# Two interleavings in a one-core hybrid layer: RWKV's triangular inverse for two tiles in step, and SSD's second state product and transposes back in another place

## The chip, the cores and the metric

The kernel runs on one core of a Trainium2 chip. The metric is the device time of one execution in microseconds; the time before is the median of three runs. The engines are TensorE (PE, with its weight loads shown apart as PEld), VectorE (DVE), ScalarE (ACT), GpSimd (POOL) and SyncE (SP), which here issues most DMAs.

## The reference, cut to what matters

One layer with three parallel token mixers on x of 256 tokens by 2048 channels, all in float32. Each mixer reads one combined projection of x; the branches are gated, merged, projected and normalised. The change touches two of the mixers:

```python
def ssd_chunked(xh, dt, a, bm, cm):              # 8 groups, 2 chunks of 128 tokens
    ...
    cb = jnp.einsum('bclgn,bcsgn->bcgls', cc, bc)
    y_diag = jnp.einsum('bcgls,bgjcls,bcsgjp->bclgjp', cb, lmat, x)
    ...
    states = jnp.einsum('bclgn,bgjcl,bclgjp->bcgjpn', bc, decay_states, x)
    ...
    y_off = jnp.einsum('bclgn,bcgjpn,bgjcl->bclgjp', cc, states, jnp.exp(cs))
    return (y_diag + y_off).reshape(b, s, h, p)

def rwkv7_recurrence(r, w, k, v, a, bvec):       # 16 heads of 64, one step for each token
    def step(state, inp):
        r_t, w_t, k_t, v_t, a_t, b_t = inp
        sa = jnp.einsum('bhvk,bhk->bhv', state, a_t)
        state = (state * w_t[:, :, None, :] + sa[..., None] * b_t[:, :, None, :]
                 + v_t[..., None] * k_t[:, :, None, :])
        return state, jnp.einsum('bhvk,bhk->bhv', state, r_t)
```

In SSD, the group's y is then multiplied with silu(z), normalised over the group's 256 channels and scaled.

## The kernel before, in words

Every large product is split into three: the weights arrive as float32 halves of 512 KB (raw), ACT rounds them to hi (L344), VectorE forms lo (L346), and TensorE adds hi*xhi, hi*xlo and lo*xhi in PSUM (L417 to L419 in proj, 48 matmuls of 128x256 for a column tile). These projections form a nearly unbroken stream on TensorE, in the order of two hand-written lists, PROG (RWKV, gates, u) and PROG2 (SSD, S5, the branches). All other products of the mixers are put between them by the Tile scheduler, which orders each engine's instructions by priority (the order of the program, or above it with high_priority) as they become ready in its own timing; on the chip each engine then follows that order. issue_after adds an edge: what it covers is issued behind a given instruction of the same engine.

RWKV works on 16 heads in four batches; a batch has two tiles (i) of two heads (h), 256 tokens in four chunks of 64. For each chunk a unit triangular 64x64 matrix is inverted. Its 32x32 diagonal blocks are inverted on VectorE (rwkv_tinv, 31 steps), go through DRAM (Td) and come back as TTf (L685). The off-diagonal block is made of three steps on TensorE, each copied out of PSUM by ACT: rwkv_ty1 transposes one diagonal block into py (L698), rwkv_ty2 copies it to Y (L709), multiplies with Aoff (L712), copies (L713), multiplies with the other diagonal block (L716), and copies into TTf (L717). py is one PSUM tile, one bank, for each i; the scheduler keeps TensorE and ACT apart on the same bank, in program order. Before the change Y has one buffer, so tile 1 follows tile 0. rwkv_chunks then walks through the four chunks (L731, X by L733, L735, L737, L741 and so on).

SSD works on eight groups (S0 to S7 in PROG2). ssd_group projects xs0, xs1, B and C, convolves them on VectorE, and then makes: cb = B*C and a transpose of B (p1), xt, the transposes of xs (p2), the state st = BT*xdec (p3, first half, L924), copied to ST by ACT (L926), the product C*ST (p3, second half, L927), read by VectorE into off, the products y of the masked M with xdt (p4, L942), the gate and the norm on VectorE and ACT (L945 to L955), and yT, four transposes of y (p6, L959), which ACT scales into ya (L961). p1, p2, p3, p4 and p6 come in this order from one PSUM ring, tag "s", of two buffers.

Of the kernel before, what the change touches and what calls it, by code (L numbers as in the profile page):

```python
# [8 lines left out]
F32 = mybir.dt.float32  # L9
F32R = mybir.dt.float32r  # L10
AF = mybir.ActivationFunctionType
ALU = mybir.AluOpType
# [4 lines left out]
T = 256  # L17
# [187 lines left out]
def emit(tc, I, O, parts=("rwkv", "s5", "ssd", "final"), dbg=None):  # L205
    nc = tc.nc
    ctx = ExitStack()
    with ctx:
# [23 lines left out]
        for st in PROG:  # L232
# [6 lines left out]
            elif st[0] == "T":  # L239
                rwkv_tinv(g, bts[int(st[1:])], int(st[1:]))  # L240
            elif st[0] == "Y":
                b = int(st[1:])
# [201 lines left out]
NCH = T // CL  # L444
# [244 lines left out]
HS = [(slice(64 * h, 64 * h + 32), slice(64 * h + 32, 64 * h + 64)) for h in range(2)]  # L689
# [11 lines left out]


def rwkv_ty2(g, bt, b, pys):
    nc, rp = g.nc, g.rp
    for i in range(2):
        py = pys[i]
        Y = rp.tile([128, 2, NCH, 32], F32, name=f"Yl{b}_{i}", tag="Yl", bufs=1)
        for lo, hi in HS:
            nc.scalar.activation(Y[lo, 0], py[lo, 0], AF.Copy)  # L709
        for lo, hi in HS:  # L710
            for c in range(NCH):
                nc.tensor.matmul(py[hi, 1, c, :], lhsT=bt.Aoff[lo, i, c, :], rhs=Y[lo, 0, c, :], start=True, stop=True)  # L712
            nc.scalar.activation(Y[hi, 1], py[hi, 1], AF.Copy)  # L713
        for h, (lo, hi) in enumerate(HS):
            for c in range(NCH):
                nc.tensor.matmul(py[lo, 2, c, :], lhsT=Y[hi, 1, c, :], rhs=bt.TTf[hi, h, i, c, 32:64], start=True, stop=True)  # L716
            nc.scalar.activation(bt.TTf[lo, h, i, :, 32:64], py[lo, 2], AF.Copy)  # L717


def rwkv_chunks(g, bt, b):  # L720
# [68 lines left out]
LC = 128  # L789
# [62 lines left out]
def ssd_z(g, zp):  # L852

    nc = g.nc
    ps = [g.pp.tile([128, 512], F32, name=f"zq{zp}_{tk}", tag="pj", bufs=3) for tk in range(2)]
    for kb in range(4):
        hi, lo = g.loadw(g.I["wza"][4 * zp + kb], f"za{zp}_{kb}")
        for k in range(4):
            kk = 4 * kb + k
            f0, l0 = kk == 0, kk == NK - 1  # L860
            for tk in range(2):
                t = slice(128 * tk, 128 * tk + 128)
                nc.tensor.matmul(ps[tk], lhsT=g.xhi[:, kk, t], rhs=hi.k512(k), start=f0, stop=False)  # L863
                nc.tensor.matmul(ps[tk], lhsT=g.xhi[:, kk, t], rhs=lo.k512(k), start=False, stop=False)  # L864
                nc.tensor.matmul(ps[tk], lhsT=g.xlo[:, kk, t], rhs=hi.k512(k), start=False, stop=l0)  # L865
    g.zs = g.cz(f"zs{zp}")
    with g.tc.high_priority():
        for tk in range(2):
            nc.scalar.activation(g.zs[:, tk, :], ps[tk], AF.Tanh, scale=0.5)
            nc.vector.scalar_tensor_tensor(g.zs[:, tk, :], g.zs[:, tk, :], 1.0, ps[tk], ALU.add, ALU.mult)  # L870


def ssd_group(g, gr):
    nc, tc = g.nc, g.tc
    cv = []
    for n, t in (("xs0", 2 * gr), ("xs1", 2 * gr + 1), ("B", 16 + gr), ("C", 24 + gr)):
        ps = g.proj(f"x{t}")
        a = g.cv(f"{n}_{gr}")
        with tc.high_priority():
            nc.scalar.activation(a, ps, AF.Identity, scale=g.p("cw", 96 + t), bias=g.p("cb", t))  # L880
            for d in (1, 2, 3):
                nc.vector.scalar_tensor_tensor(a[:, d:T], ps[:, 0:T - d], g.p("cw", 32 * (3 - d) + t), a[:, d:T], ALU.mult, ALU.add)
        th = g.kp.tile([128, T], F32, name=f"th{n}_{gr}", tag="th", bufs=2)
        nc.scalar.activation(th, a, AF.Tanh)
        nc.vector.scalar_tensor_tensor(a, th, 1.0, a, ALU.add, ALU.mult)
        cv.append(a)
    if gr % 2 == 0:
        ssd_z(g, gr // 2)
    zs = g.zs[:, :, 256 * (gr % 2):256 * (gr % 2) + 256]
    xs, B, C = cv[0:2], cv[2], cv[3]  # L890
    idn = g.c("ident")
    hs = slice(4 * gr, 4 * gr + 4)
    csb = []
    for c in range(2):
        t = g.k2(f"csb{c}_{gr}", (128, 4, LC))
        nc.sync.dma_start(t, g.csd[hs, LC * c:LC * c + LC].unsqueeze(0).to_broadcast([128, 4, LC]))
        csb.append(t)

    p1 = g.pp.tile([128, 3, LC], F32, name=f"cb{gr}", tag="s", bufs=2)
    for c in range(2):  # L900
        w = slice(LC * c, LC * c + LC)
        nc.tensor.matmul(p1[:, c, :], lhsT=B[:, w], rhs=C[:, w], start=True, stop=True)
    nc.tensor.transpose(p1[:, 2, :], B[:, 0:LC], idn)
    BT = g.k1(f"BT{gr}", (128, LC))
    nc.scalar.activation(BT, p1[:, 2, :], AF.Copy)
    CBm = g.k1(f"CBm{gr}", (128, 2, LC))
    nc.vector.tensor_tensor(CBm, p1[:, 0:2, :], g.c("mC").unsqueeze(1).to_broadcast([128, 2, LC]), ALU.mult)

    p2 = g.pp.tile([128, 2, 4, 64], F32, name=f"xt{gr}", tag="s", bufs=2)
    for c in range(2):  # L910
        for q in range(2):
            nc.tensor.transpose(p2[:, c, 2 * q:2 * q + 2, :].rearrange("p a b -> p (a b)"), xs[q][:, LC * c:LC * c + LC], idn)
    xdt = g.k2(f"xdt{gr}", (128, 2, 4, 64))
    nc.vector.tensor_tensor(xdt, p2, g.csT[:, 1, :, hs].unsqueeze(3).to_broadcast([128, 2, 4, 64]), ALU.mult)
    y = g.k2(f"y_{gr}", (128, 2, 4, 64))
    nc.vector.tensor_tensor(y, p2, g.dskb[:, hs].unsqueeze(1).unsqueeze(3).to_broadcast([128, 2, 4, 64]), ALU.mult)
    dec = g.kp.tile([128, 4], F32, name=f"dec{gr}", tag="dec", bufs=2)
    nc.vector.tensor_tensor(dec, csb[0][:, :, LC - 1], g.csT[:, 0, 0, hs], ALU.subtract)
    nc.scalar.activation(dec, dec, AF.Exp)
    xdec = g.k1(f"xdec{gr}", (128, 4, 64))  # L920
    nc.vector.tensor_tensor(xdec, xdt[:, 0], dec.unsqueeze(2).to_broadcast([128, 4, 64]), ALU.mult)

    p3 = g.pp.tile([128, 2, T], F32, name=f"st{gr}", tag="s", bufs=2)
    nc.tensor.matmul(p3[:, 0, :], lhsT=BT, rhs=xdec.rearrange("p a b -> p (a b)"), start=True, stop=True)  # L924
    ST = g.k1(f"ST{gr}")
    nc.scalar.activation(ST, p3[:, 0, :], AF.Copy)  # L926
    nc.tensor.matmul(p3[:, 1, :], lhsT=C[:, LC:T], rhs=ST, start=True, stop=True)  # L927
    off = g.k1(f"off{gr}", (128, 4, 64))
    nc.vector.tensor_tensor(off, p3[:, 1, :].rearrange("p (a b) -> p a b", a=4), g.ecs[:, hs].unsqueeze(2).to_broadcast([128, 4, 64]), ALU.mult)
    nc.vector.tensor_tensor(y[:, 1], y[:, 1], off, ALU.add)  # L930

    M = csb
    for c in range(2):
        E = csb[c]
        for h in range(4):
            nc.scalar.activation(E[:, h, :], E[:, h, :], AF.Relu, scale=-1.0, bias=g.csT[:, 0, c, 4 * gr + h:4 * gr + h + 1])
        nc.scalar.activation(E, E, AF.Exp, scale=-1.0)
        nc.vector.tensor_tensor(E, E, CBm[:, c, :].unsqueeze(1).to_broadcast([128, 4, LC]), ALU.mult)
    p4 = g.pp.tile([128, 2, 4, 64], F32, name=f"y{gr}", tag="s", bufs=2)
    for c in range(2):  # L940
        for h in range(4):
            nc.tensor.matmul(p4[:, c, h, :], lhsT=M[c][:, h, :], rhs=xdt[:, c, h, :], start=True, stop=True)  # L942

    y = y.rearrange("p c a b -> p c (a b)")
    nc.vector.tensor_tensor(y, y, p4.rearrange("p c a b -> p c (a b)"), ALU.add)  # L945
    nc.vector.tensor_tensor(y, y, zs, ALU.mult)
    ss = g.kp.tile([128, 2], F32, name=f"ss{gr}", tag="ss", bufs=2)
    sq = g.k1(f"sq{gr}")
    for c in range(2):
        nc.scalar.activation(sq, y[:, c, :], AF.Square, accum_out=ss[:, c:c + 1])  # L950
    rs = g.kp.tile([128, 2], F32, name=f"rs{gr}", tag="rs", bufs=2)
    nc.scalar.activation(rs, ss, AF.Sqrt, scale=1.0 / 256, bias=g.ssdeps)
    nc.vector.reciprocal(rs, rs)
    for c in range(2):
        nc.scalar.activation(y[:, c, :], y[:, c, :], AF.Identity, scale=rs[:, c:c + 1])  # L955
    p6 = g.pp.tile([128, 2, T], F32, name=f"yT{gr}", tag="s", bufs=2)
    for q in range(2):
        for c in range(2):
            nc.tensor.transpose(p6[:, q, LC * c:LC * c + LC], y[:, c, 128 * q:128 * q + 128], idn)  # L959
    for q in range(2):  # L960
        nc.scalar.activation(g.ya[2 * gr + q], p6[:, q, :], AF.Identity, scale=g.p("nw", 2 * gr + q))  # L961

# [427 lines left out]
```

## Time and profile before

| | |
|---|---|
| median of 3 runs | 1308.43 us (1305.89 to 1310.21) |
| profiled execution, its own time | 1302.54 us |
| its span, first to last instruction | 1300.6 us |
| TensorE busy | 1268.7 us (98%), 10916 matmuls |
| TensorE weight loads busy | 1195.2 us (92%) |
| VectorE busy | 995.7 us (77%) |
| ACT busy | 768.5 us (59%) |
| mean granted TensorE clock | 0.997 |
| chain that ended last | PE 80%, DVE 7%, ACT 6%, DMA 3% |

Matmuls overlap in the pipeline, so the duration of one (0.28 us for 128x256) is longer than the distance from its start to the next one's; for what a matmul costs in a stream, starts are to be compared. An f32 product counts as two matmul instructions. In the rows, "x8" is the number of instructions merged into one row, and a bracket tells the idle time of the engine before the row and what ended it.

### The profile page before, as it was taken

What the parts mean: (1) busy time and instruction counts of PE and PEld (TensorE: products, weight loads), DVE (VectorE), ACT (ScalarE), POOL (GpSimd) and SP (SyncE); (2) the same over time, 40 slices, a digit from 0 to 9 for tenths busy, and PEclk for the clock granted to TensorE, in tenths of its full rate; (3) what the DMA queues carried; (4) which work ended last, traced back from release to release, by engine and by line L of the source; (5) the groups of instructions that cost most, each with busy time, mean ns of one, the idle gap of its engine ahead of it and who ended that gap; (6) DMA issues with size and microseconds to landing.
All of it is one profiled execution on the core that took longest, in us unless ns stands there. A gap on an engine that the chain in (4) does not pass through costs nothing.

```text
span 1300.6 us, 27378 instructions
## 1 busy us (share of the span) xinstructions
PE 1268.7 (98%) x10916; PEld 1195.2 (92%) x10916; DVE 995.7 (77%) x1823; ACT 768.5 (59%) x1379; POOL 14.8 (1%) x72
## 2 busy tenths in 40 slices
PE   8999999999999999989999999999999999999996
PEld 8999999999989889889989989999999999999885
DVE  6779987669959857889999867999597565448655
ACT  6676555577555657885756766766454454444530
POOL 2000000000000000000000000000000000000000
PEclk9999999999999999999999999999999999999998
DMA  8655655444564554555555556456655656677751
GB/s 313 181 169 173 187 174 167 139 124 145 166 177 152 168 183 132 159 186 164 178 163 180 170 178 195 146 158 192 193 171 164 193 179 211 209 230 243 255 167 65
DMA packets 97039, 230.71 MB, mean 177 GB/s; under 512 B 26736, under 2 KB 41616, under 8 KB 96912
## 3 DMA queue, kind: packets, MB, share of 16 engines
q1 hardware_dynamic: 96336, 227.60, 57.1%
q8 instruction: 86, 1.41, 0.5%
q10 hardware_dynamic: 576, 1.36, 0.3%
q14 instruction: 41, 0.34, 0.1%
HBM read 224.37 MB, written 3.24 MB: 175 GB/s over the span
## 4 chain that ended last, share of the span: by engine, by line
PE 80%; DVE 7%; ACT 6%; DMA 3%; issue 2%; SPq 1%; DVEq 0%; POOL 0%; ACTq 0%; POOLq 0%
PE ps_g L418 6%; PE ps_g L417 6%; PE ps_g L419 6%; PE br L1235 4%; PE br L1234 4%; PE br L1236 4%; PE ps_x L417 3%; PE ps_x L418 3%; PE ps_x L419 3%; PE po L1337 2%; PE po L1338 2%; PE po L1339 2%; PE zq L865 2%; PE zq L864 2%; PE zq L863 2%
## 5 line engine op out<-in xcount | busy, mean ns | idle before, releaser
L417 PE MATMUL ps_g<-xhi,hi_g 128*128 128x256 f32 x768 | 215.2, 280 | 0.0
L418 PE MATMUL ps_g<-xlo,hi_g 128*128 128x256 f32 x768 | 215.1, 280 | 0.0
L419 PE MATMUL ps_g<-xhi,lo_g 128*128 128x256 f32 x768 | 213.8, 278 | 0.0
L346 DVE TENSOR_TENSOR lo_g<-raw_g,hi_g 128x1024 fp32r<-128x1024 f32 x96 | 117.5, 1224 | 66.6 <-ACT hi_g L344 61.9
L344 ACT ACTIVATE hi_g<-raw_g 128x1024 fp32r<-128x1024 f32 x96 | 101.5, 1058 | 93.8 <-PE ps_g L418 71.4
L418 PEld LDWEIGHTS ps_g<-xlo,hi_g 128*128 128x128 f32 x768 | 144.6, 188 | 2.0 <-issue 1.0
L417 PEld LDWEIGHTS ps_g<-xhi,hi_g 128*128 128x128 f32 x768 | 144.6, 188 | 0.9
L417 PE MATMUL ps_x<-xhi,hi_x 128*128 128x256 f32 x512 | 144.6, 282 | 0.6 <-ACT sq L950 0.6
L419 PEld LDWEIGHTS ps_g<-xhi,lo_g 128*128 128x128 f32 x768 | 144.2, 188 | 0.5
L418 PE MATMUL ps_x<-xlo,hi_x 128*128 128x256 f32 x512 | 143.9, 281 | 0.0
L419 PE MATMUL ps_x<-xhi,lo_x 128*128 128x256 f32 x512 | 143.6, 280 | 0.0
L344 ACT ACTIVATE hi_b<-raw_b 128x1024 fp32r<-128x1024 f32 x64 | 67.8, 1059 | 75.8 <-PE br L1235 43.9
L346 DVE TENSOR_TENSOR lo_x<-raw_x,hi_x 128x1024 fp32r<-128x1024 f32 x64 | 78.3, 1223 | 27.1 <-ACT hi_x L344 27.1
L417 PEld LDWEIGHTS ps_x<-xhi,hi_x 128*128 128x128 f32 x512 | 96.3, 188 | 1.6 <-ACT sq L950 0.8
L419 PEld LDWEIGHTS ps_x<-xhi,lo_x 128*128 128x128 f32 x512 | 96.3, 188 | 0.9 <-issue 0.2
L418 PEld LDWEIGHTS ps_x<-xlo,hi_x 128*128 128x128 f32 x512 | 96.3, 188 | 0.7 <-issue 0.2
L346 DVE TENSOR_TENSOR lo_b<-raw_b,hi_b 128x1024 fp32r<-128x1024 f32 x64 | 78.8, 1231 | 21.6 <-ACT hi_b L344 19.6
L344 ACT ACTIVATE hi_x<-raw_x 128x1024 fp32r<-128x1024 f32 x64 | 67.5, 1055 | 39.7 <-PE ps_x L418 23.2
L1234 PE MATMUL br<-yh0h,hi_b 128*128 128x256 f32 x256 | 72.0, 281 | 0.7 <-DVE sg L1297 0.7
L1235 PE MATMUL br<-yh0l,hi_b 128*128 128x256 f32 x256 | 72.3, 283 | 0.0
L1236 PE MATMUL br<-yh0h,lo_b 128*128 128x256 f32 x256 | 71.7, 280 | 0.0
L676 DVE TENSOR_TENSOR Pm<-TT,AT 128x16 f32<-128x16 f32 (+30 forms) x124 | 50.8, 410 | 11.6 <-POOL AT L672 5.8
(446 smaller groups left out, 3872.9 us busy)
## 6 DMA issues: line engine op xcount, KB each, us to landing
raw_g<-in_wt SPq DMA_DIRECT2D x96, 512.0 KB, 4.4
raw_x<-in_wt SPq DMA_DIRECT2D x64, 512.0 KB, 4.2
raw_za<-in_wza SPq DMA_DIRECT2D x32, 512.0 KB, 3.8
raw_b<-in_wba SPq DMA_DIRECT2D x32, 512.0 KB, 4.5
raw_wo<-in_wout SPq DMA_DIRECT2D x32, 512.0 KB, 4.7
raw_k<-in_wt SPq DMA_DIRECT2D x16, 512.0 KB, 4.8
raw_r<-in_wt SPq DMA_DIRECT2D x16, 512.0 KB, 4.1
raw_v<-in_wt SPq DMA_DIRECT2D x16, 512.0 KB, 3.8
```

The lines of the kernel that those rows point to most:

```text
L344: nc.scalar.activation(hi, raw, AF.Copy)
L346: nc.vector.tensor_tensor(lo, raw, hi.bitcast(F32), ALU.subtract)
L417: m.append(nc.tensor.matmul(ps, lhsT=hi.k(k), rhs=g.xhi[:, k, :], start=(k == 0), stop=False))
L418: m.append(nc.tensor.matmul(ps, lhsT=hi.k(k), rhs=g.xlo[:, k, :], start=False, stop=False))
L419: m.append(nc.tensor.matmul(ps, lhsT=lo.k(k), rhs=g.xhi[:, k, :], start=False, stop=(k == NK - 1)))
L676: nc.vector.tensor_tensor(Pm[:, :, 0:n], TT[:, :, 0:n], col, ALU.mult)
L863: nc.tensor.matmul(ps[tk], lhsT=g.xhi[:, kk, t], rhs=hi.k512(k), start=f0, stop=False)
L864: nc.tensor.matmul(ps[tk], lhsT=g.xhi[:, kk, t], rhs=lo.k512(k), start=False, stop=False)
L865: nc.tensor.matmul(ps[tk], lhsT=g.xlo[:, kk, t], rhs=hi.k512(k), start=False, stop=l0)
L1234: nc.tensor.matmul(ps, lhsT=hi.k(k0 + k), rhs=h, start=(k == 0), stop=False)
L1235: nc.tensor.matmul(ps, lhsT=hi.k(k0 + k), rhs=l, start=False, stop=False)
L1236: nc.tensor.matmul(ps, lhsT=lo.k(k0 + k), rhs=h, start=False, stop=(k == n - 1))
```

## The change

In rwkv_ty2 the loops are turned inside out: each of the five steps (copy, product, copy, product, copy) runs over both tiles and both halves before the next step begins. The second tile's Y takes its buffer from the ring "sq2" (two buffers, otherwise used by ysq and zt). In the products the chunk loop is outside and the halves alternate inside. In ssd_group the product C*ST (L927) and what reads it come behind the products of y, with issue_after. The transposes yT of a group and their two ACT copies are made by a function kept in g.late and called in the next group, right behind the transpose of B; group 7 makes its own at once.

```diff
 def rwkv_ty2(g, bt, b, pys):
     nc, rp = g.nc, g.rp
+    Ys = [rp.tile([128, 2, NCH, 32], F32, name=f"Yl{b}_{i}", tag=("Yl", "sq2")[i], bufs=1 + i) for i in range(2)]
     for i in range(2):
-        py = pys[i]
-        Y = rp.tile([128, 2, NCH, 32], F32, name=f"Yl{b}_{i}", tag="Yl", bufs=1)
         for lo, hi in HS:
-            nc.scalar.activation(Y[lo, 0], py[lo, 0], AF.Copy)
+            nc.scalar.activation(Ys[i][lo, 0], pys[i][lo, 0], AF.Copy)
+    for i in range(2):
+        for c in range(NCH):
+            for lo, hi in HS:
+                nc.tensor.matmul(pys[i][hi, 1, c, :], lhsT=bt.Aoff[lo, i, c, :], rhs=Ys[i][lo, 0, c, :], start=True, stop=True)
+    for i in range(2):
         for lo, hi in HS:
-            for c in range(NCH):
-                nc.tensor.matmul(py[hi, 1, c, :], lhsT=bt.Aoff[lo, i, c, :], rhs=Y[lo, 0, c, :], start=True, stop=True)
-            nc.scalar.activation(Y[hi, 1], py[hi, 1], AF.Copy)
+            nc.scalar.activation(Ys[i][hi, 1], pys[i][hi, 1], AF.Copy)
+    for i in range(2):
+        for c in range(NCH):
+            for h, (lo, hi) in enumerate(HS):
+                nc.tensor.matmul(pys[i][lo, 2, c, :], lhsT=Ys[i][hi, 1, c, :], rhs=bt.TTf[hi, h, i, c, 32:64], start=True, stop=True)
+    for i in range(2):
         for h, (lo, hi) in enumerate(HS):
-            for c in range(NCH):
-                nc.tensor.matmul(py[lo, 2, c, :], lhsT=Y[hi, 1, c, :], rhs=bt.TTf[hi, h, i, c, 32:64], start=True, stop=True)
-            nc.scalar.activation(bt.TTf[lo, h, i, :, 32:64], py[lo, 2], AF.Copy)
+            nc.scalar.activation(bt.TTf[lo, h, i, :, 32:64], pys[i][lo, 2], AF.Copy)
...
-    nc.tensor.transpose(p1[:, 2, :], B[:, 0:LC], idn)
+    m = nc.tensor.transpose(p1[:, 2, :], B[:, 0:LC], idn)
+    if gr:
+        g.late(m.ins)
...
-    nc.tensor.matmul(p3[:, 1, :], lhsT=C[:, LC:T], rhs=ST, start=True, stop=True)
-    off = g.k1(f"off{gr}", (128, 4, 64))
-    nc.vector.tensor_tensor(off, p3[:, 1, :].rearrange("p (a b) -> p a b", a=4), g.ecs[:, hs].unsqueeze(2).to_broadcast([128, 4, 64]), ALU.mult)
-    nc.vector.tensor_tensor(y[:, 1], y[:, 1], off, ALU.add)
...
-            nc.tensor.matmul(p4[:, c, h, :], lhsT=M[c][:, h, :], rhs=xdt[:, c, h, :], start=True, stop=True)
+            my = nc.tensor.matmul(p4[:, c, h, :], lhsT=M[c][:, h, :], rhs=xdt[:, c, h, :], start=True, stop=True)
+    with tc.issue_after(my.ins):
+        nc.tensor.matmul(p3[:, 1, :], lhsT=C[:, LC:T], rhs=ST, start=True, stop=True)
+    off = g.k1(f"off{gr}", (128, 4, 64))
+    nc.vector.tensor_tensor(off, p3[:, 1, :].rearrange("p (a b) -> p a b", a=4), g.ecs[:, hs].unsqueeze(2).to_broadcast([128, 4, 64]), ALU.mult)
+    nc.vector.tensor_tensor(y[:, 1], y[:, 1], off, ALU.add)
...
+    if gr < 7:
+        g.late = lambda m: ssd_back(g, gr, y, m)
+    else:
+        ssd_back(g, gr, y, None)
+
+
+def ssd_back(g, gr, y, m):
+    nc, idn = g.nc, g.c("ident")
     p6 = g.pp.tile([128, 2, T], F32, name=f"yT{gr}", tag="s", bufs=2)
-    for q in range(2):
-        for c in range(2):
-            nc.tensor.transpose(p6[:, q, LC * c:LC * c + LC], y[:, c, 128 * q:128 * q + 128], idn)
+    with g.tc.issue_after(m) if m is not None else ExitStack():
+        for q in range(2):
+            for c in range(2):
+                nc.tensor.transpose(p6[:, q, LC * c:LC * c + LC], y[:, c, 128 * q:128 * q + 128], idn)
     for q in range(2):
         nc.scalar.activation(g.ya[2 * gr + q], p6[:, q, :], AF.Identity, scale=g.p("nw", 2 * gr + q))
```

## Rows read from the trace of the kernel before

**Rows 1.** The page, part 1: busy time, share, instructions.

```profile
PE 1268.7 (98%) x10916; PEld 1195.2 (92%) x10916; DVE 995.7 (77%) x1823; ACT 768.5 (59%) x1379; POOL 14.8 (1%) x72
```

**Rows 2.** TensorE's waits: for whom, us in total, times, longest.

```profile
PE yT L959 <- ACT y L955: 4.1, 5, 1.3
PE py L698 <- DMA TTf<-Td: 4.1, 4, 1.7
...
PE st L927 <- ACT ST L926: 2.7, 1, 2.7
...
PE br L1234 <- DVE B L882: 1.3, 1, 1.3
```

**Rows 3.** TensorE's timeline (start, us, instruction) around one group of the inverse, batch 2.

```profile
377.52 0.28 PE L419 MATMUL ps_u<-xhi,lo_u 128*128 128x256 f32 x1
377.63 0.28 PE L417 MATMUL ps_u<-xhi,hi_u 128*128 128x256 f32 x1
377.84 0.43 PE L716 MATMUL py<-TTf,Yl 32*32 32x32 f32 x8
378.20 0.39 PE L418 MATMUL ps_u<-xlo,hi_u 128*128 128x256 f32 x1
378.42 0.28 PE L419 MATMUL ps_u<-xhi,lo_u 128*128 128x256 f32 x1
```

**Rows 4.** Tile py: instructions, ns min/median/max, first and last start, shape.

```profile
L712 PE MATMUL py<-Yl,Aoff x128: 191/191/212, 167.3 to 472.1; 32*32 32x32 f32 x128
```

**Rows 5.** ACT's timeline between two groups of batch 2.

```profile
375.23 0.27 ACT L713 ACTIVATE Yl<-py 32x128 f32<-32x128 f32 x1 [1.42 <-PE py L712]
```

**Rows 6.** TensorE's timeline around L698, batch 1.

```profile
237.13 0.69 PE L698 MATMUL py<-cst,TTf 32*32 32x32 f32 x32
237.75 0.39 PE L419 MATMUL ps_k<-xhi,lo_k 128*128 128x256 f32 x1
```

**Rows 7.** TensorE's timeline, chunk 0 of batch 2: pieces of L735.

```profile
387.34 0.34 PE L735 MATMUL ch<-X,TTf 128*64 128x64 f32 x4
387.60 0.43 PE L712 MATMUL py<-Yl,Aoff 32*32 32x32 f32 x8
...
393.87 0.33 PE L735 MATMUL ch<-X,TTf 128*64 128x64 f32 x2
```

**Rows 8.** TensorE's timeline around group 4's transposes back.

```profile
727.96 0.33 PE L959 MATMUL yT<-cst,y 128*128 128x128 f32 x1 [0.97 <-ACT y L955]
728.05 0.36 PE L417 MATMUL ps_x<-xhi,hi_x 128*128 128x256 f32 x1
...
728.49 0.49 PE L959 MATMUL yT<-cst,y 128*128 128x128 f32 x3
728.73 0.37 PE L417 MATMUL ps_x<-xhi,hi_x 128*128 128x256 f32 x1
```

**Rows 9.** TensorE's timeline, group 5: transpose of B, xt, the stream.

```profile
734.49 0.27 PE L903 MATMUL cb<-cst,B 128*128 128x128 f32 x1
734.60 0.60 PE L912 MATMUL xt<-cst,xs 128*128 128x128 f32 x4
734.95 0.37 PE L418 MATMUL ps_x<-xlo,hi_x 128*128 128x256 f32 x1
735.16 0.28 PE L419 MATMUL ps_x<-xhi,lo_x 128*128 128x256 f32 x1
```

**Rows 10.** TensorE's timeline, group 5: y and the second state product.

```profile
742.97 0.94 PE L942 MATMUL y<-xdt,csb 128*128 128x64 f32 x7
...
744.87 0.59 PE L927 MATMUL st<-ST,C 128*128 128x256 f32 x2
```

**Rows 11.** Windows: stretch, length, busy time of PE, PEld, DVE, ACT, POOL, granted clock.

```profile
300.00:360.00 60.00, 60.00 (x549) 57.67 (x548) 56.96 (x115) 37.73 (x67) 1.71 (x6) 1.00 0.55 163
...
560.00:600.00 40.00, 34.36 (x288) 33.42 (x286) 38.90 (x119) 29.93 (x55) 0.21 (x2) 1.00 0.49 154
```

**Rows 12.** VectorE's timeline, group 5: the last reader of cb.

```profile
738.56 0.41 DVE L907 TENSOR_TENSOR CBm<-cb,cst 128x256 f32<-128x256 f32 x1
```

## The prediction

> **What bounds the kernel now.** I read the page's first part first. TensorE is busy for 1268.7 of 1300.6 us, and its weight loads for 1195.2 us [rows 1]. Little time can therefore be won by ending idle stretches, and any larger gain must come from matmul time. The list of TensorE's waits shows which idle stretches touch the change: 4.1 us before the transposes back of SSD (yT, five times), 2.7 us before one second state product (st at L927), and 4.1 us before the first step of the RWKV inverse, which waits for a DMA [rows 2]. Then I read TensorE's timeline around one small group of the inverse. In the stream of projections one matmul starts every 0.11 us. The last one before the group is followed after 0.21 us, the group of eight takes 0.36 us to the next projection, and that one takes 0.22 us [rows 3]. The profile calls all of this busy, but a group costs (0.21-0.11) + 0.36 + (0.22-0.11) = 0.57 us of the stream. This hidden price of an interruption is what the first half of the change is about.
>
> **RWKV, removed.** L712 issues 128 TensorE instructions [rows 4], two for an f32 matmul, and L716, which makes as many products, the same. I followed them through all four batches: they come as 16 + 16 groups of eight, one for each tile, half and batch, because each group waits for an ACT copy out of the same PSUM tile. The copy at 375.23, for example, takes 0.27 us [rows 5], and the group behind it starts at 377.84 [rows 3]; projections fill the 2.3 us between. Standing alone, 32 groups cost 32 x 0.57 = 18.2 us. By my count 11 of them stand directly beside other small products, as the L712 group right after L735 at 387.60 does [rows 7]; those share an entry and a return, 11 x 0.21 = 2.3 us. That leaves 15.9 us.
>
> **RWKV, added.** Both tiles and both halves now go through each step together, so a batch needs one run of 32 instructions for L712 and one for L716. The nearest row is L698, which is of the same shape, in the same alternation of halves, and is already issued as 32: 0.62 us to the next projection [rows 6], with the entry of 0.10 and the return of 0.11 from above 0.83 us. Eight such runs cost 6.6 us. If the scheduler splits each run by tile, there are 16 groups of 16; at L698's rate a group of 16 still takes about 0.36 us, so 16 x 0.57 = 9.1 us. The saving lies between 6.8 and 9.3 us; I take 8.0, since nothing in the rows says which split it will be. A copy more in a row (four instead of one, 4 x 0.27 = 1.1 us) still fits into the 2.3 us that the stream fills.
>
> One rule of the Trainium skill disagrees with the row: "TensorE: Matmul & The Clock Gate" (section "Wait — 56ns, not 53.3ns?") says that starts never come closer than about 25 ns, however small the matmul. L698's 32 in 0.62 us are 19 ns each. By the rule 256 instructions would take at least 6.4 us instead of 8 x 0.62 = 5.0, and the gain would be 1.4 us smaller.
>
> **RWKV, what moves.** In each batch, chunk 0's L735 now comes in three pieces (x4, x2, x2), because the second tile's inverse ends later [rows 7]; in step, it should be one. A piece of two takes 0.26 us by itself and up to 0.21 more for entry and return. Eight extra pieces are worth 0 to 3.8 us; as most stand beside another group, I take 0.2 us each, 1.6 us. The second tile's Y takes its space from the ring of ysq and zt: it may wait for the preceding batch's normalisation, but nothing of TensorE's stream waits for it, so I cost this at nothing; without projections to fill, each batch would lose the 2.3 us of one step, 9 us in all. The new Y's ACT copies keep their number and shape.
>
> **SSD, transposes back (seven groups).** Their waits: 4.1 us in five places. The one of 0.50 us in group 2 (584.00) I do not count, because the next thing TensorE meets there is a 1.3 us wait for VectorE (B L882) [rows 2], and VectorE is busy for 38.9 of the 40 us from 560 to 600 [rows 11]: what is saved would be waited for there. In the other four places the y of the group is ready well before the next group's cb, except in group 0 (within a us); of their 3.6 us I count 3.0. Matmul time: one transpose, a projection with its return, three transposes and another return take 0.09 + 0.24 us [rows 8] and twice a return of 0.10 [rows 9], 0.53 us. Behind the transpose of B, four of them should take what the four of xt take, 0.35 us, but xt will then have its own return of 0.10 us [rows 9], so 0.45. That is 7 x 0.08 = 0.6 us, which I set to nothing. Their two ACT copies move along; no DMA moves in either half.
>
> **SSD, a new wait.** Now cb, BT's transpose and xt are issued in one run [rows 9]. The PSUM ring "s" has two buffers. With yT allocated between cb and xt, xt must wait until cb or yT has been read. cb's last reader, CBm on VectorE, ended at 738.97, 4.5 us after BT's transpose at 734.49 [rows 9, 12]. If projections fill this, it costs nothing; if xt blocks TensorE in all seven groups, 7 x 4.5 = 31.5 us. Of waits with one hop like this, the second state product's is the nearest row: one of eight groups stalled, for 2.7 us [rows 2]. I take 7 x 2.7 / 8 = 2.4 us. xt's late start moves the group's y too, which next waits until a group later, so that hides.
>
> **SSD, the second state product.** In group 5 it already follows the products of y, by 1 us [rows 10]; moving it directly behind saves at most a return of 0.10 us in eight groups, and nothing where ST is late. The 2.7 us stall at 566.32 is caused by ACT, inside the stretch where VectorE is the limit. I count 0 (bounds 0 and 0.8 + 2.7 = 3.5). It holds its PSUM buffer a little longer; the y products needed xt's buffer before and still do.
>
> **Sum.** -8.0 - 1.6 - 3.0 + 2.4 = -10.2 us. The profiled execution took 1302.5 us (span 1300.6), 5.9 us under the median of the runs shown (1305.9 to 1310.2). The difference should hold for either: a profiled execution of 1292 and a median of 1298.2 us.
>
> **The rivals.**
> More is won: no new wait (-2.4) and the group 2 stalls go as well (2.7 + 0.5), because RWKV's chains end sooner and S5's setup on VectorE can start sooner. For it: TensorE idles 5.6 of the 40 us there [rows 11]. Against: VectorE has no room there. 1308.4 - 15.8 = 1292.6 us.
>
> Given back: TensorE reaches batch 2's first step sooner by two batches' saving, (8.0 + 1.6) / 2 = 4.8 us, but the inverse before it runs on VectorE, busy for 57.0 of 60 us from 300 to 360 [rows 11], and its DMA is already waited for [rows 2]. The wait would grow by 4.8 us; another 3 us, the stalls counted out of yT, return at VectorE's next late copy. 1308.4 - 10.2 + 7.8 = 1306.0 us. Against it: the DMA issues stand in the same queue as the weights, which moves with TensorE.
>
> Slower: xt blocks TensorE for its PSUM buffer. It decides from a mean of (10.2 + 2.4) / 7 = 1.8 us in each of seven groups; at the full 4.5 us, 31.5 in all, the time is 1308.4 - 12.6 + 31.5 = 1327 us, and at the 2.7 us of the one stall seen, 18.9 in all, 1314.7 us. For it: both readers stand in busy queues. Against: in this trace xt, st and the y products never waited. "TensorEngine Tiling (Array Packing)", section "PSUM Bottleneck", in the Trainium skill, warns of just this: faster TensorE work leaves evacuating PSUM as the limit.
>
> **How the numbers follow.** The forecast has 0.55 (own range 1293 to 1303: the two RWKV splits, 0 to 3.8 for the pieces, one stall more or less). More won: 0.13. Given back: 0.20, of which 0.06 is still over the line. Slower: 0.12. What a measurement can tell is about 0.3%, 3.9 us, so the line is 1304.5 us. Faster 0.55 + 0.13 + 0.06 = 0.74, same 0.14, slower 0.12. The range 1289 to 1309 takes in the first three cases with half a step beside them, and leaves out the slower one and a tail below, under 2 in 10.
>
> **What would show it.** L712 and L716 in 8 to 16 runs instead of 32, and L735 of chunk 0 in one run; no TensorE wait for y before yT except in the last group; xt some microseconds behind BT's transpose, with projections between. The prediction is wrong if TensorE waits before xt, if the waits for TTf's DMA grow past 4.1 us, or if the scheduler, which draws the whole order anew, opens waits that are in none of these places.

## Result, and the profile after

The changed kernel took 1294.8 us (median of 4 runs, 1293.0 to 1297.5) against 1308.6 us beside it; the ratio is 0.9898, interval 0.9874 to 0.9923. On 1308.6 us that is 13.3 us less (10.1 to 16.5). Forecast were 1298.2 us and 10.2 us less. The profiled execution after took 1295.5 us, 7.0 us less than the profiled one before. Why the two differences are not the same is one of the questions further down.

The page of after, part 1 (busy time, share, instructions), answers to [rows 1]:

```profile
PE 1263.9 (98%) x10916; PEld 1194.1 (92%) x10916; DVE 994.8 (77%) x1823; ACT 768.7 (59%) x1380; POOL 14.7 (1%) x72
```

TensorE is still the engine that is busy nearly all the time, 4.8 us less than before. TensorE's waits after (for whom, us in total, times, longest) answer to [rows 2]:

```profile
PE s5pk L1161 <- ACT s5WT L1157: 4.3, 2, 3.9
...
PE zq L870 <- DVE lo_za L346: 2.6, 1, 2.6
PE py L698 <- DMA TTf<-Td: 1.8, 2, 1.6
```

The waits for yT, for st and for B on VectorE have left the head of the list, and the wait for TTf's DMA fell from 4.1 to 1.8 us. Two others, s5pk (new) and zq (0.4 us before), stand in their place. No line has xt.

TensorE's timeline after, around one step of the inverse in batch 0, which the scheduler left whole, and one in batch 1, which it split, answers to [rows 3, 6]:

```profile
170.05 0.28 PE L576 MATMUL lops<-xlh,wls 128*128 128x256 f32 x1
170.26 0.69 PE L713 MATMUL py<-Yl,Aoff 32*32 32x32 f32 x32
170.88 0.38 PE L576 MATMUL lops<-xll,wls 128*128 128x256 f32 x1
171.11 0.28 PE L576 MATMUL lops<-xlh,wls 128*128 128x256 f32 x1
...
227.72 0.44 PE L713 MATMUL py<-Yl,Aoff 32*32 32x32 f32 x16
...
228.75 0.44 PE L713 MATMUL py<-Yl,Aoff 32*32 32x32 f32 x16
```

Entry 0.21, 32 instructions in 0.62 us, return 0.23: just what L698 showed before. The split run adds an entry and a return. Through all batches the two products (L713 and L720) now come in 10 runs instead of 32. Tile py after (instructions, ns, first and last start) answers to [rows 4]:

```profile
L713 PE MATMUL py<-Yl,Aoff x128: 191/191/212, 170.3 to 420.3; 32*32 32x32 f32 x128
L720 PE MATMUL py<-TTf,Yl x128: 191/191/212, 174.5 to 423.3; 32*32 32x32 f32 x128
```

The last of them starts at 420.3 us, before at 472.1 [rows 4]: the chain of the last batch ends about 50 us sooner, far more than the matmul time that was saved. The pieces of L735 (now L741) in chunk 0 of batch 2 [rows 7] have become one:

```profile
372.23 0.45 PE L741 MATMUL ch<-X,TTf 128*64 128x64 f32 x8
```

TensorE's timeline after in group 5 of SSD, with the projections between left out, answers to [rows 8 to 10]:

```profile
719.74 0.27 PE L909 MATMUL cb<-cst,B 128*128 128x128 f32 x1
719.85 0.60 PE L977 MATMUL yT<-cst,y 128*128 128x128 f32 x4
...
723.02 0.60 PE L920 MATMUL xt<-cst,xs 128*128 128x128 f32 x4
...
728.23 1.89 PE L946 MATMUL y<-xdt,csb 128*128 128x64 f32 x16
...
731.64 0.59 PE L948 MATMUL st<-ST,C 128*128 128x256 f32 x2
```

yT follows the transpose of B at once, xt comes 3.2 us later, and projections fill the time: no idle time stands before xt. The last reader of cb on VectorE, CBm, began at 721.15 us and took 0.41 us [rows 12]; xt comes 1.5 us behind it. The second state product follows the products of y by 1.5 us; before it was 1 us [rows 10]. Windows after (stretch, length, busy PE, PEld, DVE, ACT, POOL with their instructions, granted clock, DMA share, GB/s) answer to [rows 11], with another stretch ahead:

```profile
460.00:540.00 80.00, 77.42 (x597) 71.67 (x597) 66.60 (x167) 59.37 (x116) 0.11 (x1) 0.98 0.52 159
560.00:600.00 40.00, 36.09 (x308) 35.33 (x308) 34.58 (x76) 27.49 (x62) 0.32 (x3) 0.96 0.51 153
```

From 560 to 600 us VectorE has 34.6 us of work where it had 38.9 [rows 11]: part of it was done between 460 and 540 us, where it now has 66.6 us (56.9 before).

### The profile page after: what moved, and what is told of

Same layout as the page of the kernel before. It is cut to its first block, busy times and chain, and to the rows that moved or that the text cites. A ratio compares the mean times of both kernels' runs of the same rounds, so it can differ in the third digit from the quotient of the medians.

```text
span 1293.7 us, 27392 instructions
## 1 busy us (share of the span) xinstructions
PE 1263.9 (98%) x10916; PEld 1194.1 (92%) x10916; DVE 994.8 (77%) x1823; ACT 768.7 (59%) x1380; POOL 14.7 (1%) x72
## 4 chain that ended last, share of the span: by engine, by line
PE 85%; DVE 6%; ACT 4%; DMA 2%; issue 1%; SPq 0%; DVEq 0%; ACTq 0%
PE ps_g L419 6%; PE ps_g L418 6%; PE ps_g L417 6%; PE br L1253 4%; PE br L1252 4%; PE br L1254 4%; PE ps_x L417 4%; PE ps_x L418 4%; PE ps_x L419 4%; PE po L1357 2%; PE po L1355 2%; PE po L1356 2%; PE zq L870 2%; PE zq L869 2%; PE zq L871 2%
```

## Experiments

Each ratio is against runs of the kernel before on the same chip (medians 1306.8, 1307.5 and 1307.3 us for the three groups of four). Differences are the ratio's distance from 1 times that median, with the interval's ends in brackets.

**Only the RWKV half.** rwkv_ty2 is that of the change; ssd_group is that of before.

> The kernel before with only the RWKV half of the change. Theory (interruptions of the projection stream): 8 to 10 runs of L712 and L716 instead of 32, L735 of chunk 0 in one run, 8 to 11 us faster than before, ratio 0.992 to 0.994. Rival (the gain of the whole change comes from the waits of SSD and from a newly drawn order, interruptions are free because the engine is only relabelled busy): within 3 us of before.

Measured: 1290.9 us, ratio 0.9875 (0.9855 to 0.9896), 16.3 us less (13.6 to 18.9). This is more than the 9.6 us of its terms and than the 8 to 11 us expected, and by the median more than the whole change gives, though the two intervals overlap.

**Only the SSD half.** rwkv_ty2 is that of before.

> The kernel before with only the SSD half. Theory: the waits for y before yT go except in the last group (3 to 4 us), xt comes some microseconds later without a wait of TensorE; 2 to 5 us faster, ratio 0.996 to 0.9985. Rival (the SSD half carries the change): 8 to 13 us faster.

Measured: 1317.1 us, ratio 1.0073 (1.0053 to 1.0093), 9.5 us more (6.9 to 12.2). Neither expectation held: the two halves have opposite signs. TensorE waits 4.3 us for zs on VectorE, as in the kernel with only the second product moved (further down), and for the split of y in branch a:

```profile
PE br L1247 <- DVE yh0l L425: 4.1, 3, 2.5
```

**The price of an interruption, by itself.** The kernel before, with 256 extra matmul instructions of the inverse's shape (on the identity, into a PSUM tile that nothing reads) between the products of branch b: once as 32 groups of eight, once as 8 groups of 32 in alternating halves. The code ahead of branch b is unchanged.

```diff
+        m = nc.tensor.matmul(ps, lhsT=hi.k(k0 + k), rhs=l, start=False, stop=False)
+        if extra is not None and k in (2, 6):
+            extra(m)
...
+    if g.nsmall % 1:          # second kernel: % 4
+        return
+    with g.tc.issue_after(m.ins):
+        for c in range(4):        # second kernel: range(8)
+            for lo, hi in HS[:1]:         # second kernel: HS[:2]
+                nc.tensor.matmul(g.dm[hi, c, :], lhsT=idn[lo, lo], rhs=idn[lo, 0:32], start=True, stop=True)
```

> The kernel before, with 32 extra groups of four f32 products of 32x32 (eight instructions, results read by nobody) put into the middle of the products of the S5 branch, where nothing waits for them. Theory: 32 x 0.57 = 18 us slower, ratio 1.014. Rival (only the instructions cost, 256 at 0.02 to 0.045 us): 5 to 11 us slower.

> The same number of extra instructions (256) in the same products, but in 8 groups of 32 with the two halves alternating. Theory: 8 x 0.83 = 6.6 us slower, ratio 1.005, so about 11.6 us faster than the 32 groups of eight. Rival (only the instructions cost): the same as the 32 groups.

Measured: 32 groups of eight 1323.7 us, ratio 1.0119 (1.0092 to 1.0146), 15.6 us more; 8 groups of 32 1311.8 us, ratio 1.0044 (1.0031 to 1.0058), 5.8 us more. The same number of instructions costs 9.8 us less in 24 interruptions fewer. TensorE's timeline of the first kernel:

```profile
1096.49 0.28 PE L1239 MATMUL br<-yh1l,hi_b 128*128 128x256 f32 x1
1096.70 0.43 PE L1286 MATMUL dm<-cst 32*32 32x32 f32 x8
1097.07 0.38 PE L1242 MATMUL br<-yh1h,lo_b 128*128 128x256 f32 x1
1097.29 0.28 PE L1238 MATMUL br<-yh1h,hi_b 128*128 128x256 f32 x1
```

and of the second:

```profile
1104.68 0.28 PE L1239 MATMUL br<-yh1l,hi_b 128*128 128x256 f32 x1
1104.89 0.69 PE L1286 MATMUL dm<-cst 32*32 32x32 f32 x32
1105.51 0.38 PE L1242 MATMUL br<-yh1h,lo_b 128*128 128x256 f32 x1
1105.74 0.28 PE L1238 MATMUL br<-yh1h,hi_b 128*128 128x256 f32 x1
```

From the projection ahead to the second one behind, less the two distances of 0.115 us that would be there anyway, a group of eight costs 0.80 - 0.23 = 0.57 us and one of 32 costs 1.06 - 0.23 = 0.83 us. These are the prediction's figures to the hundredth. The whole kernels give 0.49 and 0.73 us for each group; the 18 and 6.6 us that were expected lie inside their intervals.

The two kernels differ in one thing more: the groups of eight use one half, those of 32 alternate between two. One instruction takes 0.19 us (as in [rows 4]), so the rows of 0.43 and 0.69 us mean 0.24 us from the first start to the last in a group of eight and 0.50 us in one of 32, 34 against 16 ns from start to start. What is left, 0.57 - 0.24 and 0.83 - 0.50, is 0.33 us in both: that is the interruption by itself. Of the 11.6 us expected between the two kernels, 24 x 0.33 = 7.9 are interruptions and 3.7 come from the alternation. The change has both as well, and no run separates them.

**Only the transposes back moved.** RWKV and the second state product are those of before; g.late and ssd_back are those of the change.

```diff
-    nc.tensor.transpose(p1[:, 2, :], B[:, 0:LC], idn)
+    m = nc.tensor.transpose(p1[:, 2, :], B[:, 0:LC], idn)
+    if gr:
+        g.late(m.ins)
```

> The kernel before, with the transposes back moved into the next group and nothing else. Theory A (the moved transposes bring the last groups' ya late, so that VectorE's splits of ya pile up where branch a begins): 6 to 11 us slower than before, and the last split yh0l ends 10 us or more later after yT's start would have been. Rival B (the second state product behind y holds a PSUM buffer and delays the groups): within 3 us of before. Rival C (xt's wait for a PSUM buffer): as A, but lost evenly over the groups.

Measured: 1299.8 us, ratio 0.9945 (0.9930 to 0.9960), 7.2 us less (5.2 to 9.2). None of the three expectations held: late transposes do not harm by themselves. Of its TensorE waits one for yT is left (1.1 us; before 4.1 in five), and that for st is gone, but one for B on VectorE has grown from 1.3 to 3.0 us. Its profiled execution was the slowest of the six (1304.4 us), so where the 7.2 us come from stays open.

**Only the second state product moved.**

```diff
-    nc.tensor.matmul(p3[:, 1, :], lhsT=C[:, LC:T], rhs=ST, start=True, stop=True)
...
+    with tc.issue_after(my.ins):
+        nc.tensor.matmul(p3[:, 1, :], lhsT=C[:, LC:T], rhs=ST, start=True, stop=True)
```

> The kernel before, with the second state product behind the products of y and nothing else. Theory A: within 3 us of before. Rival B: 5 to 10 us slower. Rival C: within 3 us.

Measured: 1315.0 us, ratio 1.0057 (1.0045 to 1.0069), 7.5 us more (5.9 to 9.0). Rival B held. One stretch stands out. Group 1's y before the change, and from this kernel's trace tile ya on ACT in group 0, group 1's y and the later wait on TensorE, group 1's gate and the next zs on VectorE, and the load of csb by SP with ACT's use of it, each from the timeline:

```profile
527.52 1.89 PE L942 MATMUL y<-xdt,csb 128*128 128x64 f32 x16
```

```profile
551.60 0.82 ACT L962 ACTIVATE ya<-yT,par 128x256 f32<-128x256 f32 x2
```

```profile
555.36 1.90 PE L938 MATMUL y<-xdt,csb 128*128 128x64 f32 x16
...
567.43 0.58 PE L417 MATMUL ps_x<-xhi,hi_x 128*128 128x256 f32 x1 [5.92 <-DVE zs L870]
```

```profile
562.10 0.68 DVE L947 TENSOR_TENSOR y<-y,zs 128x512 f32<-128x512 f32 x1
...
566.70 1.27 DVE L870 SCALAR_TENSOR_TENSOR zs<-zs,zq 128x512 f32<-128x512 f32 x2
```

```profile
557.58 0.38 SPq L896 DMA_DIRECT2D csb<-csd  x1
```

```profile
562.24 1.27 ACT L932 ACTIVATE csb<-csb,csT 128x128 f32<-128x128 f32 x4 [2.53 <-DMA csb<-csd]
...
565.48 1.07 ACT L869 ACTIVATE zs<-zq 128x512 f32<-128x512 f32 x2
```

The transposes of group 0 keep one of the two buffers of ring "s" until ya(0) is written, and ya stands in memory that RWKV leaves only about then. Group 1's st has the other buffer. In the old place st is read out early and its buffer goes to y(1), which started at 527.52 us before the change. Now st keeps it until y(1) has been issued, and y(1) has to wait for ya(0)'s buffer: it starts at 555.36. No idle time stands before it, since the scheduler drew its order with the same buffers in view; that the buffer is the reason is read from the code and these starts, and no run frees the buffer alone. What is late behind y(1) is the next zs. It has one buffer, which y(1)'s gate reads until 562.78, but that is not what ended last: the load of csb for the group behind was issued only at 557.58, behind y(1)'s products, ACT sat idle 2.53 us for it, and ACT's part of zs stands behind it in ACT's queue and runs 2.7 us after the gate. TensorE waits 5.9 us for the PSUM that zs reads, and then runs slowly. Windows of the same trace (columns as before):

```profile
568.00:570.00 2.00, 2.00 (x12) 2.00 (x11) 0.78 (x3) 1.98 (x8) 0.00 (x0) 0.50 0.62 221
570.00:572.00 2.00, 2.00 (x11) 2.00 (x11) 1.14 (x9) 1.74 (x5) 0.00 (x0) 0.50 0.00 0
572.00:574.00 2.00, 2.00 (x14) 2.00 (x13) 1.20 (x11) 1.99 (x3) 0.00 (x0) 0.66 0.04 8
```

After the wait the granted clock is 0.50, the lower level, for some 6 us: 37 matmuls stand in these three windows where 60 would (20 in each 2 us from 574 us on), another 2.3 us at 0.1 us each. 5.9 + 2.3 = 8.2 us lies inside the interval of the measured loss.

**The same product moved only from group 2 on.**

```diff
+    if gr < 2:
+        nc.tensor.matmul(p3[:, 1, :], lhsT=C[:, LC:T], rhs=ST, start=True, stop=True)
+        second()
...
+    if gr > 1:
+        with g.tc.issue_after(my.ins):
+            nc.tensor.matmul(p3[:, 1, :], lhsT=C[:, LC:T], rhs=ST, start=True, stop=True)
+        second()
```

> The kernel before with the second state product behind the products of y in groups 2 to 7 only; groups 0 and 1 keep the old place. Theory (the harm sits in groups 0 and 1, while ya(0) waits for memory and keeps a PSUM buffer): within 2.5 us of the kernel before, and no wait of TensorE for zs (L870). Rival (each of eight groups pays alike, 7.5/8 each): 5.6 us over the kernel before.

Measured: 1306.0 us, ratio 0.9993 (0.9983 to 1.0003), 0.9 us less, and no wait for zs. The expectation held, but the two traces show why it could not fail: this kernel has the same instructions, by operation, tile and shape, in the same order as the kernel before, on TensorE, VectorE, ACT, GpSimd and in SP's DMA issues. In groups 2 to 7 the scheduler had the product behind those of y already; before the change only groups 0 and 1 have it ahead (493.9 us against y at 494.4, 523.7 against 527.5). So the run does not test a price for each group; with the kernel above it does show that the whole loss comes with the first two groups, the only ones in which the edit turns the product and y round. It is also a second profile of the kernel before in all but name.

**RWKV in step, and the second product moved in all groups.** The RWKV half and the edit of the second product together.

> RWKV in step, and the second state product behind the products of y; the transposes back stay at once. Theory (the second product holds its PSUM buffer until the products of y have been issued, which costs only while ya(0) keeps the other buffer, and ya(0) has its memory by about 510 us here instead of 545): the loss of 7.5 us that this part had alone shrinks to 3 us or less, so 13 to 16 us under the kernel before, and TensorE has no wait of 4 us or more for zs (L870). Rival (the later product costs in every group): the loss stays, 8 to 9 us under the kernel before.

Measured: 1291.5 us, ratio 0.9880 (0.9865 to 0.9894), 15.7 us less, and no wait for zs. Here too the edit moves next to nothing: with RWKV in step the scheduler has the product behind y in seven groups by itself and amid y's products in group 3, and group 3's is all that differs between the two orders. So the 0.6 us against RWKV alone are two runs of nearly one program, not a price. What both show is that the product behind y(1) goes without the wait for zs where ya(0) ends early (500.7 us instead of 552.4), as the theory of the held buffer has it.

**RWKV in step, and the transposes moved.** The RWKV half and the edit of the transposes together.

> RWKV in step, and of SSD only the transposes back moved into the next group; the second state product stays in its old place. Theory (it is the second product that costs, and the two other parts are gains from different causes): both gains hold, though RWKV in step already took part of the yT waits; 16 to 21 us under the kernel before, 3 us or more under RWKV alone's -16, and no wait for zs at L870. Rival (parts do not add, since the whole order is drawn anew): somewhere between -10 and -16 us, no better than RWKV alone.

Measured: 1294.1 us, ratio 0.9893 (0.9879 to 0.9908), 14.0 us less (12.0 to 15.8). The rival held: the 7.2 us that this edit gave alone are not there; the gain is 2.3 us under that of RWKV alone, with intervals that just overlap. The trace has the same instructions in the same order as the whole change, on the same engines as above: in the changed kernel the edit of the second product moves nothing, and this is the whole change measured again (14.0 and 13.3 us). Its longest wait is that of the whole change too, s5pk. From its trace, the issue of one load of csb by SP, ACT, and TensorE, each from the timeline:

```profile
558.80 0.38 SPq L902 DMA_DIRECT2D csb<-csd  x1
```

```profile
564.45 1.28 ACT L944 ACTIVATE csb<-csb,csT 128x128 f32<-128x128 f32 x4 [4.45 <-DMA csb<-csd]
...
567.68 0.58 ACT L1156 ACTIVATE s5WT<-s5pb 128x512 f32<-128x512 f32 x1
```

```profile
568.32 0.44 PE L1160 MATMUL s5pk<-s5cq,s5W 128*32 128x32 f32 x16 [5.05 <-ACT s5WT L1156]
...
570.23 0.41 PE L418 MATMUL ps_x<-xlo,hi_x 128*128 128x256 f32 x1
570.45 0.41 PE L419 MATMUL ps_x<-xhi,lo_x 128*128 128x256 f32 x1
```

csb's load is issued when group 2's products of y have freed its buffer and lands 5.6 us later. ACT reaches the instruction that needs it 4.45 us too early, and behind it in ACT's queue stands s5WT, for which TensorE waits 5.05 us. This is the late load of csb once more. Then projections start every 0.21 us instead of 0.115 (until 574.7 us), some 2 us more. In RWKV alone the scheduler had put s5WT ahead of that csb (it ran at 563.08 us), and TensorE did not wait for it. That the order of these two on ACT follows from the late transposes, and not from any other redrawing of the order, was not tried.

**Group 6's transposes left in place.** In two kernels: the SSD half alone, and the whole change, each with `if gr < 6` where the change has `if gr < 7`, so that ya(12) and ya(13), two of the last tiles that branch a waits for, are written at once.

> The SSD half alone, but group 6 makes its transposes back at once, as group 7 does; groups 0 to 5 make them in the next group. Theory A: what the SSD half lost at the start of branch a comes back, 5 to 10 us faster than the SSD half alone, so within 4 us of before. Rivals B and C (lost in every group): 1 to 2 us faster than the SSD half alone, 7 us or more slower than before.

> The whole change, but group 6 makes its transposes back at once. Theory A: 3 to 5 us faster than the whole change, so 16 to 18 us faster than before, ratio 0.986 to 0.988. Rivals B and C: as the whole change, 13 us faster than before, ratio 0.990.

Measured: the SSD half 1308.5 us, ratio 1.0009 (0.9998 to 1.0020), 1.2 us more than before and 8.3 us better than with all seven moved, as expected; the waits for yh0l are gone, the one for zs (4.9 us) stays. The whole change 1297.6 us, ratio 0.9921 (0.9908 to 0.9934), 10.3 us less: not better than as it is. So the late ya seems to cost where VectorE splits y late (yh0l); in the whole change nothing waits for yh0l, and there the expectation of a gain failed.

**RWKV in step, S5's setup held back.** The first exponential of S5's setup gets a bias of zero made from group 1's norm, and the setup is listed behind group 1; one VectorE instruction of 128x1 is added.

```diff
+    V.tensor_scalar(g.gate, g.rs1[:, 0:1], 0.0, None, ALU.mult)
+    A.activation(dt, ldt, AF.Exp, bias=g.gate)
```

> RWKV in step alone, but S5's setup is held back: its first exponential takes a bias of zero that is made from the norm of SSD's group 1 (ready at about 540 us), and its instructions are listed behind group 1. It adds one VectorE instruction of 128x1. Theory (6 us of RWKV's gain come from S5's setup on VectorE starting at 500 instead of 545 us): the gain falls from 16 to 9 to 11 us, and TensorE's waits for VectorE between 540 and 600 us come back. Rival (the gain is all in the stream's interruptions, S5's setup is cover only): the gain stays at 14 us or more.

Measured: 1295.3 us, ratio 0.9907 (0.9890 to 0.9923), 12.2 us less (10.1 to 14.4), between the two forecasts. The exponential ran at 536.1 us (500.4 in RWKV alone, 547.4 before), and TensorE's waits have this line:

```profile
PE s5pb L1148 <- DVE s5W L1136: 5.7, 1, 5.7
```

So an early S5 setup is worth about 4 us of RWKV's 16, not 6, though the intervals of the two kernels still touch.

## Why the prediction came out as it did

**The price of a group: right. The saving in RWKV: too small.** The dummy groups bear out 0.57 and 0.83 us, and the timeline of after has the forecast runs (10, forecast 8 to 16; L741 in 17 pieces, L735 before in 24). But RWKV's term as a whole was mis-sized: forecast 9.6 us, measured 16.3. In the profiled executions RWKV alone has 8.7 us less busy TensorE time (1260.0 against 1268.7), which looks like the forecast and isn't, because the two are not at the same clock. Before has a granted clock of 1.00 from 0 to 1290 us; RWKV alone has 0.83 from 160 to 170 and 0.96 from 460 to 540 us, which by the trace's record of the clock costs 4.2 us of its busy time. At the full clock it has 12.9 us less matmul time, and 3.0 us less idle time (28.9 against 31.9), 15.9 us together. The kernel with the second product, nearly the same program, has 11.6 and 4.9. So 2 to 3 us more of the stream were saved than the sum has, in products that were not taken apart, and 3 to 5 us of waits that the forecast had left to a rival.

**"The difference should hold for either": this did not hold.** RWKV alone is 11.8 us faster by profiled executions (1302.5 to 1290.7) but 16.3 by medians. The forecast took the profiled execution of before as typical. It was not: TensorE's waits there were followed by no lower clock. The kernel with 32 dummy groups is, but for the order of a few small products near 515 us, the same program up to branch b; windows of its trace, of before, and of the kernel moved from group 2 on, whose order is that of before throughout:

```profile
160.00:170.00 10.00, 7.82 (x83) 7.26 (x81) 5.09 (x7) 3.86 (x7) 0.15 (x1) 0.83 0.49 134
560.00:570.00 10.00, 7.29 (x57) 6.75 (x56) 6.64 (x28) 9.09 (x16) 0.00 (x0) 0.94 0.64 185
570.00:580.00 10.00, 10.00 (x79) 9.91 (x78) 10.00 (x39) 6.71 (x12) 0.10 (x1) 0.89 0.44 141
```

```profile
160.00:170.00 10.00, 8.05 (x98) 7.56 (x97) 6.39 (x10) 5.71 (x10) 0.15 (x1) 1.00 0.60 168
560.00:570.00 10.00, 7.29 (x61) 7.01 (x60) 8.90 (x45) 9.42 (x19) 0.10 (x1) 1.00 0.47 134
570.00:580.00 10.00, 10.00 (x90) 10.00 (x90) 10.00 (x29) 7.76 (x14) 0.00 (x0) 1.00 0.47 159
```

```profile
160.00:170.00 10.00, 7.74 (x81) 7.25 (x80) 4.58 (x9) 3.70 (x7) 0.16 (x1) 0.83 0.50 131
```

The idle time is the same (7.29 us busy from 560 to 570 in the first two), but the clock behind it is 0.94 and 0.89 instead of 1.00, and 11 matmuls fewer stand from 570 to 580. Summed over the three stretches, (0.17 + 0.06 + 0.11) x 10 = 3.4 us of clock are lost. Group 7's transpose of B comes at 814.8 us there, at 813.2 with the eight groups, at 813.1 in the kernel moved from group 2 on, and at 810.3 in the profile of before. RWKV in step alone shows the same 0.83 in the first stretch, and 1.00 in the other two, where it has no wait for st. Its own profile (1290.7 us) lies at its median (1290.9); that of before was spared some 3 us. Of the seven other traces with RWKV's half as before, five have 0.83 from 160 to 170 us. That most runs of before are not spared is inferred from these traces and from the medians.

**Given back, and more won.** The wait for TTf's DMA shrank, so nothing was given back there; the rival that put 4.8 us on it was wrong. The mechanism of the rival in which more is won is real: the chains end 50 us sooner, S5's setup begins at 501.1 instead of 547.4 us, and the waits for st and B go. The argument against it, that VectorE has no room from 560 to 600 us, missed that the work itself would leave that stretch. With the setup held back, about 4 us are lost.

**Transposes back.** As forecast, none of the seven waits any more, but xt doesn't wait either, so the +2.4 was not there. The -3.0 did not come: with RWKV in step only 2.1 us of waits for yT were left to win, and the order that the scheduler drew for the late transposes has a wait of 4.3 us for s5pk, where ACT stands in front of a late load. This is the last of the prediction's own signs of being wrong, a wait in none of the places that it named. Alone the edit gives 7.2 us; behind RWKV's it costs 2.3 and 3.0 us in the two measurements of this kernel, each with an interval that overlaps that of RWKV alone. The sentence that no DMA moves in either half was true of the edit and not of the order drawn from it.

**Second state product: 0 came out, for another reason.** The prediction named only gains (0 to 3.5 us) and passed over the buffer in one sentence, that it is held "a little longer". It had looked at group 5, where the product already stands behind y; in groups 0 and 1 it did not, and there the move alone costs 7.5 us while group 0's transposes hold the ring's other buffer. In the whole change the term is 0 because the edit moves nothing: with RWKV in step the scheduler puts the product there by itself, at a time when that buffer is free.

**Luck.** RWKV's term was too small by 6.7 us (9.6 against 16.3). The SSD half, forecast at 0.6 us less, took back 3.0 behind RWKV's, too good by 3.6. The two errors have opposite signs, and that the time came within 3.4 us of the forecast is owed to this.

**Slower, by xt.** It did not happen: projections fill the 3.2 us. The SSD half alone is slower, as that rival's sign was, but with the waits behind the st buffer and the late splits in branch a, neither of them in the prediction.

RWKV's half alone, at 1290.9 us, is the fastest by its median, 2 to 3 us ahead of the whole change, though the intervals overlap; the second product's edit is idle there, and the transposes had better stay.

## What to carry to other kernels

Where small matmuls cut into a full stream, count the interruptions as well as the instructions: here each cost 0.33 us beside its instructions, and those followed each other twice as fast in alternating halves. Before moving a reader of a ring buffer, ask who holds the other buffers at the worst time of the program, not in the group at which the trace was opened. Forecast each half of a change with the waits that the other half leaves: here the SSD edits alone gave -7.2 and +7.5 us, and behind RWKV's edit +2 to +3 and 0. And compare the order of two traces before you call an edit tested: where a scheduler draws the order, an edit can move nothing or next to nothing, as in three of these kernels.

## What the runs showed of the hardware

Waits of TensorE can cost more than their length. In the changed kernel the wait of 2.58 us for lo_za is followed by windows at these clocks (columns as before):

```profile
532.00:534.00 2.00, 0.83 (x4) 0.70 (x5) 2.00 (x6) 1.43 (x3) 0.00 (x0) 1.00 0.00 0
534.00:536.00 2.00, 2.00 (x7) 1.58 (x6) 2.00 (x4) 1.98 (x6) 0.00 (x0) 0.57 0.82 240
536.00:538.00 2.00, 2.00 (x7) 1.56 (x6) 2.00 (x6) 1.38 (x3) 0.00 (x0) 0.58 0.69 190
538.00:540.00 2.00, 2.00 (x11) 1.60 (x10) 2.00 (x8) 0.11 (x1) 0.00 (x0) 1.00 0.84 281
```

The clock falls to the lower of its two levels (1.2 of 2.4 GHz) here only after work has begun again at 533.2 us, and products of 128x512 then start every 0.43 us instead of 0.23; after the 5.9 us wait for zs it was down already when work began at 567.43 (0.63 from 566 to 568 us). The 2.7 us wait for st in the profile of before had no such tail, while the kernel with 32 dummy groups had one behind the same wait (2.5 us there). And the same order of instructions ran at 1.00 in one execution and at 0.83 in another from 160 to 170 us. The Trainium skill, "TensorE: Matmul & The Clock Gate", section "What's actually happening", says of the start of a kernel that the number of matmuls at the lower level differs between runs of the same kernel; these traces show such a difference in the middle of one. The section "HAM oscillation — how this bites in real kernels" of the same page of the Trainium skill tells of DMA waits that put the engine back to half rate; here waits for VectorE and ACT of 2.6 to 5.9 us do the same.
